# Other shapes for the paired tiles of a decoder trunk: halves and steps of 256, -64 and 64 bytes

## The chip, the cores and the metric

The kernel runs on one core of a Trainium2 chip. The metric is the device time of one execution in microseconds (us). Times are medians of several runs; the profile comes from one more execution, whose own time is given beside its span.

## What is computed

The reference is a decoder trunk of two layers over 256 tokens of width 2048. Each layer has a token mixer (a convolution module in the first, stick-breaking attention with 16 heads in the second) and a gated network with a causal depthwise convolution of width 3. Cut to what matters:

```python
def stick_breaking_mixer(h, qkv_w, o_w):
    ...
    o = stick_breaking_attention(qkv[0], qkv[1], qkv[2])
    o = o.transpose(0, 2, 1, 3).reshape(bsz, t_len, d)
    return o @ o_w

def conv_ffn(h, up_w, dw_w, dw_b, down_w):
    u = causal_depthwise_conv(h @ up_w, dw_w, dw_b)
    gt, val = jnp.split(u, 2, axis=-1)
    return (jax.nn.silu(gt) * val) @ down_w

def reference(x, c, ...):
    for i in range(DEPTH):
        ...
        x = x + gate * y
        ...
        x = x + gate * conv_ffn(h, ffn_up_w[i], ffn_dw_w[i], ffn_dw_b[i], ffn_down_w[i])
    return rms_norm(x, final_norm_g)
```

The inner width of the gated networks is 5632, that is 44 blocks of 128; the model width is 16 blocks of 128. All data are float32.

## The kernel before

Activations are kept transposed: a block is 128 channels (partitions) by 256 tokens. A product runs over a list of pairs (output block, inner block) in an order that `plan` writes out; weights come in pieces of 8 such blocks of 128 x 128 (`load_next`, a 512 KB DMA into `raw`), and `split_next` splits each piece into a rounded high part `wh` (ScalarE) and a remainder `wl` (VectorE), both in the type float32r that TensorE multiplies in one pass.

The activations are split in the same way into a high half and a low half. A product is then high x high + low x high + high x low. In `gemm` there are two forms. Without `both`, there are three matmuls of 256 columns for each weight block (L302 to L304). With `both`, the two halves of the activation tile are read as one moving operand of 2 x 256 columns against `wh` (L298), and the high half alone, 256 columns, against `wl` (L299): a pair. The weight block is loaded anew ahead of each matmul.

The halves lie in one tile. `h_tiles` and `halved` lay them out: `HP = T + 8 = 264` numbers from the start of one half to that of the next, 528 numbers (2112 bytes) for a tile. Four kinds of tiles come from `halved`: `z` (input of the second product of the convolution module, L943, read in triples), `g` of either network (input of the down products, L999), and `o` (one for each head, L1127). The `h` tiles come from `h_tiles`.

The g tiles of a network live in a pool of their own, opened in `ffn`, with 23 names (`NG = KF // 2 + 1`) for 44 inner blocks: block j takes the name `g{j % 23}`. Each network runs up product, down product over blocks 0 to 21, up product, down product over blocks 22 to 43. A down product runs over 16 output blocks; the plan begins with four output blocks in turn on each inner block (all but the last four inner blocks, which then come output block by output block), then takes the other twelve one at a time over all 22 inner blocks. The output projection `o` does the same over 16 inner blocks, one for each head. Tiles of one pool lie one behind the other in the order in which they are first taken.

The v product of the attention is written apart (`v_product`, L1164 to L1166): there the h tile is the stationary operand and 512 contiguous columns of `wh` or `wl` are the moving one.

While TensorE multiplies, VectorE splits weights (L247), closes each output block (L1010, L1012) and sums the conditioning matrices of the stages to come (L336), whose rows GpSimd's queue fetches (1 MB each).

Of the kernel before, what the change touches and what calls it, by code (L numbers as in the profile page):

```python
# [11 lines left out]
F32R = mybir.dt.float32r  # L12
# [4 lines left out]
P = 128  # L17
# [7 lines left out]
LATE_POOL, LATE_PE = 10, 8  # L25
PRODUCTS = 11

HEAD = 16
UBUFS = 9
M0 = 6  # L30
# [86 lines left out]
def hybrid_trunk(ctx: ExitStack, tc: tile.TileContext, cfg: Cfg, io: dict):  # L117
    nc = tc.nc
    D, T, H = cfg.D, cfg.T, cfg.H
# [253 lines left out]
    HP = T + 8  # L373
# [7 lines left out]
    def h_pairs():  # L381
        return [pairs[k] for k in range(KD)]

    def halved(pool, name):

        v = pool.tile([P, 2 * HP], F32R, name=name).rearrange("p (a t) -> p a t", a=2)[:, :, :T]
        return v[:, 0], v[:, 1], v

    def split_act(t, hh, hl, bias=None):
# [120 lines left out]
    with ExitStack() as cv:  # L510
# [422 lines left out]
        for j in range(KD + 1):  # L933
            if j < KD:
                zt.append(t256())
                if j > 1:
                    nc.vector.tensor_tensor(ys[j], ys[j], dm, op=ALU.subtract)
                nc.vector.tensor_tensor(zt[j], ys[j], rs, op=ALU.mult)
                nc.scalar.activation(zt[j], zt[j], AF.Silu, bias=pc("ln_b", j, 1), scale=pc("ln_g", j, 1))
            if j == 1:  # L940
                low()
            if j > 0:
                zs.append(halved(zpool, f"z{j - 1}"))  # L943
                split_act(zt[j - 1], *zs[j - 1][:2])
            if j in (1, 2, 4):
                split_next()
# [18 lines left out]
    def ffn(i, entry, out):  # L965
        m = f"ffn{i}"
        NG = KF // 2 + 1
        with ExitStack() as fs:
            gpool = fs.enter_context(tc.tile_pool(name=f"g{i}", bufs=1))
            if i == 0:  # L970
                more["pool"] = fs.enter_context(tc.tile_pool(name="mods", bufs=MORE_MODS))
            gh, gl, gb = [None] * KF, [None] * KF, [None] * KF
            pend = {}

            def conv3(ps, nb, both):
                y = t256()
                if both:
                    s = t256()
                    nc.scalar.copy(s, ps[:, T:2 * T])
                    nc.vector.tensor_tensor(s, ps[:, :T], s, op=ALU.add)  # L980
                    ps = s
                w = lambda k: pc(f"fdw{i}", nb * FW + k, 1)
                nc.scalar.activation(y, ps[:, :T], AF.Identity, bias=pc(f"fdb{i}", nb, 1), scale=w(FW - 1))  # L983
                for k in range(FW - 1):
                    s = FW - 1 - k
                    nc.vector.scalar_tensor_tensor(y[:, s:], ps[:, :T - s], w(k), y[:, s:],  # L986
                                                   op0=ALU.mult, op1=ALU.add)
                return y

            def up_done(nb, ps, both=False):  # L990
                pend[nb] = conv3(ps, nb, both)
                j = nb % KF
                if not (j in pend and j + KF in pend):
                    return
                yg, yv = pend.pop(j), pend.pop(j + KF)
                s = t256()
                nc.scalar.activation(s, yg, AF.Silu)
                nc.vector.tensor_tensor(s, s, yv, op=ALU.mult)
                gh[j], gl[j], gb[j] = halved(gpool, f"g{j % NG}")  # L999
                nc.scalar.copy(gh[j], s)  # L1000
                nc.vector.tensor_tensor(gl[j], s, gh[j].bitcast(F32), op=ALU.subtract)

            def down_done(h):
                def done(nb, ps):
                    if nb < KD - 2:
                        t = t256()
                        nc.scalar.activation(t, ps[:, T:2 * T], AF.Copy, scale=gate(m, nb))  # L1007
                        nc.gpsimd.tensor_tensor(xs[nb], xs[nb], t, op=ALU.add)  # L1008
                    else:
                        nc.vector.scalar_tensor_tensor(xs[nb], ps[:, T:2 * T], gate(m, nb), xs[nb],  # L1010
                                                       op0=ALU.mult, op1=ALU.add)
                    nc.vector.scalar_tensor_tensor(xs[nb], ps[:, :T], gate(m, nb), xs[nb],  # L1012
                                                   op0=ALU.mult, op1=ALU.add)
                    if h == 1 and i == 0:
                        out.add(nb)
                    elif h == 1:
                        out.add(xs[nb])
                        nc.scalar.activation(xs[nb], xs[nb], AF.Copy, scale=pc("fin_g", nb, 1))
                return done

            hh, hl = entry.product(f"up{i}0a", up_done, "silu_and_others")
            both = h_pairs() if i else None
            rest = (lambda nb, ps: up_done(nb, ps, True)) if i else up_done
            gemm(f"up{i}0b", hh, hl, rest, banks=[psum_b, psum_a], both=both)
            gemm(f"up{i}1a", hh, hl, rest, both=both)
            need(m, 2)
            gemm(f"down{i}0", gh, gl, down_done(0), both=gb)
            gemm(f"up{i}1b", hh, hl, rest, both=both)
            act_tables("sqrt_and_others")
            gemm(f"down{i}1", gh, gl, down_done(1), quiet=QUIET, both=gb)  # L1030
            drain(fill)
# [37 lines left out]
    with ExitStack() as at:  # L1069
# [12 lines left out]
        def attention(h):  # L1082
            q, k, v, vc = qk[h], qk[H + h], vs[h // GH], (h % GH) * P
            yield
            zp = (psum_acc if h == 1 else psum_a)()
            nc.tensor.matmul(zp[:, 0:T], k[:, 0:P], q, start=True, stop=True)
            nc.tensor.matmul(zp[:, T:CO], k[:, P:2 * P], q[:, P:2 * P], start=True, stop=True)
            z = zp[:, :CO]
            e = t2.tile([P, CO], F32, name="e", bufs=3)
            nc.scalar.activation(e, z, AF.Abs)  # L1090
            nc.scalar.activation(e, e, AF.Exp, scale=-1.0)
            lg = t2.tile([P, CO], F32, name="lg")
            nc.scalar.activation(lg, e, AF.Ln, bias=one_c)
            mk = t2.tile([P, CO], F32, name="e", bufs=3)
            nc.vector.scalar_tensor_tensor(mk, z, 0.0, lg, op0=ALU.max, op1=ALU.add)
            nc.vector.scalar_tensor_tensor(lg, z, 0.0, lg, op0=ALU.min, op1=ALU.subtract)
            for c0 in (0, T):
                nc.gpsimd.affine_select(out=mk[:, c0:c0 + P], in_=mk[:, c0:c0 + P], pattern=[[1, P]],
                                        compare_op=ALU.is_gt, fill=0.0, base=0, channel_multiplier=-1)
            if h < 2:  # L1100
                yield
            mh = t2.tile([P, CO], F32R, name="mh", bufs=1)
            ml = t2.tile([P, CO], F32R, name="ml", bufs=1)
            yield
            with tc.high_priority(offset=PRIORITY):
                nc.scalar.copy(mh, mk)
                nc.vector.tensor_tensor(ml, mk, mh.bitcast(F32), op=ALU.subtract)
            yield
            yield
            sp = psum_b()  # L1110
            nc.tensor.matmul(sp[:, :CO], tri_r, mh, start=True, stop=False)
            nc.tensor.matmul(sp[:, :CO], tri_r, ml, start=False, stop=False)
            nc.tensor.matmul(sp[:, P:T], ones_r, mh[:, T:CO], start=False, stop=False)
            nc.tensor.matmul(sp[:, P:T], ones_r, ml[:, T:CO], start=False, stop=True)
            nc.vector.tensor_tensor(lg, lg, sp[:, :CO], op=ALU.subtract)
            a = t2.tile([P, CO], F32, name="e", bufs=3)
            nc.scalar.activation(a, lg, AF.Exp)
            for c0 in (0, T):
                nc.gpsimd.affine_select(out=a[:, c0:c0 + P], in_=a[:, c0:c0 + P], pattern=[[1, P]],
                                        compare_op=ALU.is_gt, fill=0.0, base=0, channel_multiplier=-1)  # L1120
            yield
            yield
            op = psum_b()
            nc.tensor.matmul(op[:, 0:P], v[:, 0, vc:vc + P], a[:, 0:P], start=True, stop=True)
            nc.tensor.matmul(op[:, P:T], v[:, 0, vc:vc + P], a[:, P:T], start=True, stop=False)
            nc.tensor.matmul(op[:, P:T], v[:, 1, vc:vc + P], a[:, T:CO], start=False, stop=True)
            oh[h], ol[h], ob[h] = halved(apool, f"o{h}")  # L1127
            with tc.high_priority(offset=PRIORITY):
                nc.scalar.copy(oh[h], op[:, :T])
                nc.vector.tensor_tensor(ol[h], op[:, :T], oh[h].bitcast(F32), op=ALU.subtract)  # L1130
# [210 lines left out]
```

## Time and profile before

| | |
|---|---|
| time, median of 3 runs | 2302.11 us (2302.03 to 2304.25) |
| time of the profiled execution | 2302.23 us |
| its span, first to last instruction | 2300.5 us |
| matmuls in the trace | 14378 |
| L298 on h, g, o tiles | 1760, 1408, 256 |
| L299 on h, g, o tiles | 1760, 1408, 256 |
| DMA | 603.14 MB, mean 262 GB/s |

How to read it: PE is TensorE's matmuls, PEld its weight loads, DVE VectorE, ACT ScalarE, POOL GpSimd, SP the engine that issues the weight DMAs. Rows of groups and of windows give busy time and counts. The duration that the profile gives for one matmul covers more than the distance to the next one's start, as matmuls overlap in the array; the distance from start to start is what adds up to the time of a stage. A row such as "387/394/406" gives the shortest, the median and the longest duration in ns. A row of the windows view begins with the stretch in us from the start of the span and its length, then busy time and count for each engine asked for, the granted clock, the share of the DMA engines' time and GB/s.

### The profile page before, as it was taken

Reading aid. Unit: us, or ns where it says so; the run is one execution under the profiler, and the core shown is the slowest. Engines: PE = TensorE matmul, PEld = TensorE weight load, DVE = VectorE, ACT = ScalarE, POOL = GpSimd, SP = SyncE. Lnnn points to the kernel's source line nnn. Section 1 sums busy time; section 2 is a strip of 40 time slices with the busy share of each in tenths; the row PEclk is TensorE's granted clock in tenths of the full one; section 3 lists DMA queues with packets and bytes.
Section 4 is the critical chain, followed back from the end, with each engine's and each line's share of the span. In section 5 each row is a group of like instructions: output and inputs, shape, how many; then the busy total and the mean of one; then the engine's idle time right before and its main releaser. Section 6 shows DMA issues by size and latency. Waiting matters only on the chain.

```text
span 2300.5 us, 37664 instructions
## 1 busy us (share of the span) xinstructions
PE 2266.0 (98%) x14378; PEld 2012.9 (87%) x14378; DVE 1791.2 (78%) x2508; ACT 1219.9 (53%) x1930; POOL 406.2 (18%) x534
## 2 busy tenths in 40 slices
PE   7999999999999999999999999999999999999997
PEld 5888678999998999998888888888888888888886
DVE  7689968889998899999975555779899655777654
ACT  2056655755544455555465555657555544555553
POOL 4058713200003100003311100112000010000031
PEclk9999999999999999999999999999999999999999
DMA  9988799788899989898755555566777666666663
GB/s 396 416 327 311 268 368 361 267 301 336 332 339 347 332 329 343 334 332 320 265 184 160 165 173 171 168 188 234 240 281 275 194 191 186 190 184 191 189 188 110
DMA packets 139143, 603.14 MB, mean 262 GB/s; under 512 B 15441, under 2 KB 15569, under 8 KB 115153
## 3 DMA queue, kind: packets, MB, share of 16 engines
q1 hardware_dynamic: 120242, 464.42, 57.9%
q0 software_dynamic: 18720, 136.32, 16.0%
q8 instruction: 112, 1.84, 0.3%
q14 instruction: 69, 0.57, 0.1%
HBM read 598.58 MB, written 2.10 MB: 261 GB/s over the span
## 4 chain that ended last, share of the span: by engine, by line
PE 88%; DVE 5%; DMA 4%; ACT 1%; issue 1%; POOL 0%; DVEq 0%; SPq 0%; ACTq 0%; POOLq 0%
PE ps L298 33%; PE ps L299 17%; PE ps L302 9%; PE ps L303 8%; PE ps L304 8%; PE ps L678 5%; DMA mraw<-in_mt_mix 3%; DVE mraw L336 2%; DVE wl L247 1%; PE ps L1164 1%; PE ps L1165 1%; PE ps L1166 1%; PE ps L591 1%; PE auxa L591 1%; DMA mraw<-in_mt_ffn 1%
## 5 line engine op out<-in xcount | busy, mean ns | idle before, releaser
L247 DVE TENSOR_TENSOR wl<-raw,wh 128x1024 fp32r<-128x1024 f32 x688 | 849.0, 1241 | 297.7 <-ACT wh L243 295.9
L243 ACT CAST wh<-raw 128x1024 fp32r<-128x1024 f32 x688 | 719.3, 1047 | 661.7 <-PE ps L298 301.6
L298 PE MATMUL ps<-h,wh 128*128 128x512 f32 x1760 | 619.0, 394 | 0.0
L299 PE MATMUL ps<-h,wl 128*128 128x256 f32 x1760 | 493.7, 281 | 0.0
L298 PE MATMUL ps<-g,wh 128*128 128x512 f32 x1408 | 493.2, 394 | 0.0
L302 PE MATMUL ps<-h,wh 128*128 128x256 f32 (+1 forms) x1504 | 421.7, 280 | 0.0
L303 PE MATMUL ps<-h,wh 128*128 128x256 f32 (+1 forms) x1504 | 420.5, 280 | 0.0
L304 PE MATMUL ps<-h,wl 128*128 128x256 f32 (+1 forms) x1504 | 419.0, 279 | 0.1
L299 PE MATMUL ps<-g,wl 128*128 128x256 f32 x1408 | 395.3, 281 | 2.4 <-DVE wl L247 2.2
L298 PEld LDWEIGHTS ps<-h,wh 128*128 128x128 f32 x1760 | 330.5, 188 | 74.4
L336 DVE CUSTOM_DVE_ANT_0 mraw<-mraw,csr 128x2048 f32<-128x2048 f32 x152 | 348.7, 2294 | 42.4 <-DMA mraw<-in_mt_mix 31.0
L299 PEld LDWEIGHTS ps<-h,wl 128*128 128x128 f32 x1760 | 332.3, 189 | 0.2
L298 PEld LDWEIGHTS ps<-g,wh 128*128 128x128 f32 x1408 | 264.3, 188 | 60.4
L303 PEld LDWEIGHTS ps<-h,wh 128*128 128x128 f32 x1504 | 284.7, 189 | 0.1
L304 PEld LDWEIGHTS ps<-h,wl 128*128 128x128 f32 x1504 | 282.6, 188 | 0.7 <-DVE wl L247 0.7
L302 PEld LDWEIGHTS ps<-h,wh 128*128 128x128 f32 x1504 | 282.4, 188 | 0.2
L299 PEld LDWEIGHTS ps<-g,wl 128*128 128x128 f32 x1408 | 265.9, 189 | 4.0 <-DVE wl L247 4.0
L678 PE MATMUL ps<-h,raw 128*128 128x256 f32 x832 | 188.8, 382 | 0.0
L678 PEld LDWEIGHTS ps<-h,raw 128*128 128x128 f32 x832 | 157.8, 191 | 28.3 <-issue 6.7
L1008 POOL TENSOR_TENSOR x<-x,t 128x256 f32<-128x256 f32 x56 | 68.1, 1218 | 534.6 <-ACT t L1007 534.5
L986 DVE SCALAR_TENSOR_TENSOR t<-t,par 128x254 f32<-128x254 f32 (+1 forms) x184 | 88.8, 483 | 46.6 <-ACT t L983 43.7
L718 DVE SCALAR_TENSOR_TENSOR auxb<-u,cpar,auxb 128x256 f32<-128x256 f32 x297 | 121.6, 482 | 4.5 <-ACT auxb L702 3.8
(266 smaller groups left out, 2613.3 us busy)
## 6 DMA issues: line engine op xcount, KB each, us to landing
raw<-in_w_down SPq DMA_DIRECT2D x176, 512.0 KB, 4.4
mraw<-in_mt_ffn POOLq DMA_DIRECT2D x64, 1024.0 KB, 6.1
raw<-in_w_pw SPq DMA_DIRECT2D x96, 512.0 KB, 8.1
mraw<-in_mt_mix POOLq DMA_DIRECT2D x48, 1024.0 KB, 7.9
raw<-in_w_up01b SPq DMA_DIRECT2D x84, 512.0 KB, 6.2
raw<-in_w_up11b SPq DMA_DIRECT2D x84, 512.0 KB, 3.8
raw<-in_w_up00b SPq DMA_DIRECT2D x80, 512.0 KB, 6.2
raw<-in_w_up10b SPq DMA_DIRECT2D x80, 512.0 KB, 4.7
```

What stands on the lines that cost most here:

```text
L243: nc.scalar.copy(wh[:, :n], v[:, :n])
L247: nc.vector.tensor_tensor(wl[:, :n], v[:, :n], wh[:, :n].bitcast(F32), op=ALU.subtract)
L298: nc.tensor.matmul(o, wh[:, c], both[kt], start=first, stop=False, skip_group_check=True)
L299: nc.tensor.matmul(o[:, :T], wl[:, c], xh[kt], start=False, stop=left[nb] == 0, skip_group_check=True)
L302: nc.tensor.matmul(o, wh[:, c], xh[kt], start=first, stop=False, skip_group_check=halves > 0)
L303: nc.tensor.matmul(o, wh[:, c], xl[kt], start=False, stop=False, skip_group_check=halves > 0)
L304: nc.tensor.matmul(o, wl[:, c], xh[kt], start=False, stop=left[nb] == 0, skip_group_check=halves > 0)
L336: nc.vector.tensor_tensor_reduce(out=v, in0=v, in1=csr, scale=1.0, scalar=0.0, op0=ALU.mult, op1=ALU.add, accum_out=macc[:, nb:nb + 1])
L678: nc.tensor.matmul(banks[j][:, nb // KD * T:(nb // KD + 1) * T], w[:, b * P:(b + 1) * P], hf[kt], start=first, stop=left[j] == 0, skip_gro ...
L718: nc.vector.scalar_tensor_tensor(conv_ps[j], us[j % UBUFS][:, k:k + T], tap(j, k), conv_ps[j], op0=ALU.mult, op1=ALU.add)
L986: nc.vector.scalar_tensor_tensor(y[:, s:], ps[:, :T - s], w(k), y[:, s:], op0=ALU.mult, op1=ALU.add)
L1008: nc.gpsimd.tensor_tensor(xs[nb], xs[nb], t, op=ALU.add)
```

## The change

`halved` takes its shape from a table by kind: the distance between the halves, the size of the tile, both in numbers of 4 bytes, and how many numbers are left free ahead of the first tile of that kind. `z` keeps its numbers. `g0` (first network) has halves 256 apart in tiles of 512, with 24 left free ahead of the first; `g1` (second network) halves 264 apart in tiles of 560; `o` (heads) halves 272 apart in tiles of 544. What is written into the tiles, and what reads them, is the same.

```diff
+PAIRS = {"z": (264, 528, 0), "g0": (256, 512, 24), "g1": (264, 560, 0), "o": (272, 544, 0)}
...
-    def halved(pool, name):
-
-        v = pool.tile([P, 2 * HP], F32R, name=name).rearrange("p (a t) -> p a t", a=2)[:, :, :T]
+    ahead_of = {kind: v[2] for kind, v in PAIRS.items()}
+
+    def halved(pool, kind, name):
+
+        low, size, _ = PAIRS[kind]
+        at = ahead_of.pop(kind, 0)
+        v = pool.tile([P, at + size], F32R, name=name)[:, at:at + 2 * low].rearrange("p (a t) -> p a t", a=2)[:, :, :T]
         return v[:, 0], v[:, 1], v
...
-                zs.append(halved(zpool, f"z{j - 1}"))
+                zs.append(halved(zpool, "z", f"z{j - 1}"))
...
-                gh[j], gl[j], gb[j] = halved(gpool, f"g{j % NG}")
+                gh[j], gl[j], gb[j] = halved(gpool, f"g{i}", f"g{j % NG}")
...
-            oh[h], ol[h], ob[h] = halved(apool, f"o{h}")
+            oh[h], ol[h], ob[h] = halved(apool, "o", f"o{h}")
```

## The prediction, made before the changed kernel was built or run

> **What bounds the kernel now.** I read the page first (span, busy shares, chain), then busy time by stage, and then single matmul starts, since only those are finer than the change.
>
> ```profile
> span 2300.5 us, 37664 instructions
> PE 2266.0 (98%) x14378; PEld 2012.9 (87%) x14378; DVE 1791.2 (78%) x2508; ACT 1219.9 (53%) x1930; POOL 406.2 (18%) x534
> PEclk9999999999999999999999999999999999999999
> PE 88%; DVE 5%; DMA 4%; ACT 1%; issue 1%; POOL 0%; DVEq 0%; SPq 0%; ACTq 0%; POOLq 0%
> ```
>
> TensorE works for 98% of the span, at full granted clock in every slice, and holds 88% of the chain that ended last. Time can only fall if its matmuls start closer together. The profiled execution took 2302.23 us around its 2300.5 us span, 0.12 us over the median of the runs shown, so I sum against 2302.23 and subtract 0.12 at the end.
>
> The stages that the change touches are the two down products of the first network (rows 1 and 3 below), the output projection o of the heads (row 4) and the two down products of the second network (rows 5 and 7). Rows 2 and 6 are up products, whose h tiles stay as they are.
>
> ```profile
> core 0: us, PE busy (x) PEld busy (x) DVE busy (x) ACT busy (x) POOL busy (x), PEclk, DMA share, GB/s
> 668.14:791.33 123.19, 123.19 (x706) 107.97 (x705) 104.72 (x105) 53.51 (x61) 28.10 (x33) 1.00 0.94 348
> 791.33:1026.57 235.24, 235.24 (x2018) 235.24 (x2017) 216.91 (x276) 123.20 (x180) 16.40 (x31) 1.00 0.89 332
> 1026.57:1153.46 126.89, 124.50 (x706) 107.99 (x705) 118.47 (x131) 64.11 (x94) 43.88 (x41) 1.00 0.80 292
> 1452.90:1545.30 92.40, 92.40 (x534) 81.16 (x533) 68.93 (x86) 55.32 (x77) 19.26 (x20) 1.00 0.60 183
> 1805.48:1928.70 123.22, 123.22 (x707) 108.00 (x706) 64.03 (x67) 53.66 (x62) 14.18 (x14) 1.00 0.64 192
> 1928.70:2163.90 235.20, 235.20 (x1347) 206.35 (x1346) 169.34 (x249) 133.73 (x206) 0.00 (x0) 1.00 0.62 188
> 2163.90:2287.11 123.21, 123.21 (x706) 108.06 (x705) 59.52 (x62) 63.51 (x90) 28.41 (x28) 1.00 0.50 154
> ```
>
> A down product is 16 output blocks by 22 inner blocks, so 352 pairs of one 512-column matmul (L298, joined halves against wh) and one 256-column matmul (L299, first half against wl): 704 matmuls. 123.2 us over 352 pairs is **350.0 ns a pair**. The up product of row 6 has 42 blocks by 16, so 672 pairs in 235.20 us: 350.0 again. That of row 2 has three 256-column matmuls in place of a pair, 672 triples in 235.24 us: 350.1. So 768 columns cost 350 ns whether they come as two matmuls or three, from h or from g. The first reading is discouraging for this change: on average the time goes by columns.
>
> **Addresses do matter locally.** A joined tile is 2 x 264 numbers, 2112 bytes, which is 64 modulo 256: each next inner block starts 64 bytes further round a circle of 256. From the program's memory plan the first g tile starts at 160 modulo 256, then 224, 32, 96, 160.
>
> ```profile
> L298 PE MATMUL ps<-g,wh x1408: 387/394/406, 668.1 to 2286.8; 128*128 128x512 f32 x176
> 1808.30:1809.73 1.43, 1.43 (x11) 1.00 0.87 301
> 1809.73:1811.13 1.40, 1.40 (x11) 1.00 0.86 319
> 1811.13:1812.52 1.39, 1.39 (x11) 1.00 0.13 53
> 1812.52:1813.93 1.41, 1.41 (x11) 1.00 0.76 186
> ```
>
> The first row: the same matmul takes 387 to 406 ns. The other four are stretches of four pairs each on one tile, at 32, 96, 160 and 224 (a down product begins with four output blocks in turn on each inner block): 357.5, 350, 347.5 and 352.5 ns a pair. So a fixed address repeated has its own price, a few ns either side of 350. The DMA share runs from 0.13 to 0.87 across them without order, so transfers are not what differs.
>
> **The change part by part.** No instruction, wait or DMA is added, removed or moved; z keeps its numbers. What changes is where the g and o tiles lie, hence the price of 704 pairs with g of the first network, 704 of the second and 256 of o (16 blocks by 16). 1 ns on all 1664 pairs is 1.66 us.
>
> First network: joined halves are contiguous, tiles 2048 bytes, start 0 modulo 256 (24 numbers are put ahead of the first tile; when that name is used again in the second product it is not, a 22nd of that stage, counted like the rest). Every step from block to block is then 0 modulo 256. Nearest rows: the v product, whose moving operand is a contiguous 512 columns of wh or wl, always the same modulo 256.
>
> ```profile
> 1231.36 0.39 PE L1166 MATMUL ps<-wh,h 128*128 128x512 f32 x1
> 1231.59 0.39 PE L1164 MATMUL ps<-wh,h 128*128 128x512 f32 x1
> 1231.82 0.40 PE L1165 MATMUL ps<-wl,h 128*128 128x512 f32 x1
> 1232.05 0.39 PE L1166 MATMUL ps<-wh,h 128*128 128x512 f32 x1
> 1232.29 0.59 PE L1086 MATMUL auxa<-q,k 128*128 128x256 f32 x2
> ```
>
> Four starts in 0.93 us: 232.5 ns for 512 columns, 348.8 for 768, 1.2 under 350. Over 704 pairs **-0.8 us**. Bounds from the fixed-address rows: 347.5 (-1.8 us) to 357.5 (+5.3 us). I take the v rows because they alone are contiguous.
>
> Second network: tiles of 560 numbers, 2240 bytes, -64 modulo 256; halves as before. The trace has that step once per output block, at the return from the last inner block (224) to the first (160):
>
> ```profile
> 1805.48:1830.78 25.30, 25.30 (x145) 1.00 0.67 207
> 1836.38:1921.00 84.62, 84.62 (x486) 1.00 0.64 188
> 2194.79:2279.42 84.63, 84.63 (x487) 1.00 0.51 156
> 1851.41 0.39 PE L298 MATMUL ps<-g,wh 128*128 128x512 f32 x1
> ...
> 1851.76 0.40 PE L298 MATMUL ps<-g,wh 128*128 128x512 f32 x1
> ...
> 1852.12 0.39 PE L298 MATMUL ps<-g,wh 128*128 128x512 f32 x1
> ...
> 1852.46 0.39 PE L298 MATMUL ps<-g,wh 128*128 128x512 f32 x1
> ```
>
> The second row holds 11 whole output blocks, 242 pairs; at 350.0 it would be 84.70. It is 0.08 us short, so each of 11 steps of -64 is worth some **-6 to -7 ns** over what follows it (in the head, first row, 72 pairs with steps of 0 in 25.30 us, 351.4, the price is over 350 instead). In single starts the gain is not at the step: the pair right after it takes 0.36, the next 0.34. I carry it over as if each step were worth it: some 273 more such steps in the first down product and 268 in the second (every inner step of the twelve single output blocks, one in four in the head), 541 x 6.3 ns = **-3.4 us**. Bounds: nothing recurring (0), or the 0.36 pair at every step (read to 0.01, so between 0.35 and 0.36: +5 ns each, +2.7 us).
>
> Heads: tiles of 2176 bytes, step 128, halves 1088 bytes apart in place of 1056. The second down product of the second network goes 160, then 32, then 160 on its return (two steps of 128): 84.63 against 84.70 over 11 returns, 22 steps, -3.2 ns each; o takes some 219 such steps: **-0.7 us**. That halves 64 apart cost otherwise than halves 32 apart no row shows; ends 347.5 and 357.5 a pair give -0.6 to +1.9 us, and I take 0, because the contiguous v rows (0 apart) and the h rows (32 apart) differ by only 1.2.
>
> Whether the rest keeps up: the fullest of these stages is the second of the first network, where VectorE works 118.47 of 126.89 us and TensorE already stood still.
>
> ```profile
> PE ps L299 <- DVE wl L247: 2.2, 3, 1.1
> 1084.18 10.04 DMA mraw<-in_mt_ffn
> L1000 ACT CAST g<-t x88: 390/407/413, 440.6 to 2169.3; 128x256 fp32r<-128x256 f32 x88
> L1001 DVE TENSOR_TENSOR g<-t,g x88: 416/420/427, 441.3 to 2170.3; 128x256 fp32r<-128x256 f32 x88
> ```
>
> A 10 us transfer on the chain holds VectorE, and wl comes late three times; a faster TensorE arriving there earlier would wait longer by what it gained, at most half of the 0.8 us. In the other four stages VectorE is busy for 85% or less. The writers of the moved tiles (L1000, L1001, 0.4 us each, and the like for o) I cost at nothing: they finish well ahead of the down product that reads them, beside matmuls; if each were a tenth slower, 88 x 0.08 = 7 us on two engines with room, not on the chain.
>
> Sum: -0.8 - 3.4 - 0.7 = -4.9; 2302.23 - 4.9 - 0.12 = **2297.2 us**, 0.2% down, at the very edge of what a measurement of this kernel can tell from no change (about 0.2%, 4.6 us).
>
> [...]
>
> [...]
>
> **The rivals.**
> *Fixed by columns.* The local differences are only displaced starts that even out, as 350.0 in three kinds of stage suggests. For it: the stage rows. Against: 357.5 beside 347.5 at fixed addresses, and 242 pairs 0.08 us short twice. **2302.1 us**, band 2 us. [...]
>
> *Pieces of 64 bytes.* If the moving operand is fetched in 64-byte pieces at a fixed price, a pair before touches 17 + 16 + 17 = 50 (halves start at 32 and 0 modulo 64), so 7.0 ns each. The new first network touches 32 + 16 = 48: 336 ns, -14 x 704 = -9.9 us; o touches 51: +7 x 256 = +1.8; the second network 50. With the steps' -3.4: **2290.6 us**. For it: v touches 33 pieces, 231 against 232.5 seen. Against: nothing decisive; the aligned half of h (L303) shows no shorter stage.
>
> *A bad address.* The new address 0 lies between 224 (352.5) and 32 (357.5) in the fixed-address rows, and after the change every one of the 704 pairs repeats it. If it locks in as 32 does, +7.5 x 704 = +5.3 us, and if the -64 step keeps its 0.36 pairs, +2.7: 2302.1 + 8.0 = **2310.1 us**. It makes the kernel slower by over 0.2% once the mean pair exceeds 350 + 4.6/1.664 = 352.8. For it: 1.43. Against: the v rows, fixed at one address and contiguous, at 348.8.
>
> **How the numbers follow.** Forecast 0.42, band 2294.5 to 2300, of which 0.24 lies under 2297.5; fixed by columns 0.22; 64-byte pieces 0.22; bad address 0.14. Faster 0.24 + 0.22 = 0.46, same 0.18 + 0.22 = 0.40, slower 0.14. The range 2288 to 2306.5 leaves out most of the bad address (0.12) and the low end of the pieces (0.05).
>
> **What would show it.** Forecast: first network's down products near 348.8 ns a pair (122.8 us and, with its waits, about 126.5), second network's near 121.5 us each, o near 91.7, up products unchanged at 235.2. Columns: all at 350.0. Pieces: first network 118.3 us a product. Bad address: 125.8 us there. It would be wrong altogether if an up product changed, if the number of matmuls changed, or if VectorE's wait in the second down product grew by more than the stage gained.

## The result, and the profile after

The changed kernel takes 2305.97 us (median of 18 runs, lowest 2304.56) against 2302.70 us for the kernel before (18 runs): ratio 1.0015, 95% interval 1.0009 to 1.0021. One of the 18 runs of either kernel took 3200 us (its granted clock in the changed kernel's was 0.66); without it the medians are 2305.93 and 2302.66. The changed kernel is slower by 0.15%, inside what I had called no change (0.2%), and on the other side of the forecast of 2297.2 us.

First the page of the changed kernel: its span, the busy shares and the granted clock.

```profile
span 2304.9 us, 37664 instructions
PE 2270.7 (99%) x14378; PEld 2015.0 (87%) x14378; DVE 1791.1 (78%) x2508; ACT 1222.4 (53%) x1930; POOL 406.0 (18%) x534
PEclk9999999999999999999999999999999999999999
```

Instructions and matmuls are what they were; the granted clock was 0.997 over the span, 0.998 before; TensorE is busy for 4.7 us more (2270.7 against 2266.0). The profiled execution took 2306.58 us, the one of before 2302.23 us. Next the windows view of the changed kernel, the same seven stages as before in the same order (the columns: stretch, length, TensorE's busy time and matmuls, granted clock, DMA share, GB/s; all windows rows below have them).

```profile
core 0: us, PE busy (x), PEclk, DMA share, GB/s
669.50:793.90 124.40, 124.40 (x707) 1.00 0.93 346
793.90:1029.10 235.20, 235.20 (x2019) 1.00 0.89 331
1029.10:1156.40 127.30, 125.47 (x707) 1.00 0.80 291
1455.70:1548.10 92.40, 92.40 (x536) 1.00 0.60 183
1808.30:1932.30 124.00, 124.00 (x706) 1.00 0.63 191
1932.30:2167.50 235.20, 235.20 (x1346) 1.00 0.62 188
2167.50:2291.50 124.00, 124.00 (x706) 1.00 0.51 153
```

The up products (rows 2 and 6) have not moved. All four down products have become longer. With the stage bounds taken from the start times of single matmuls, to the nanosecond:

| stage | before, us | after, us | after, ns a pair |
|---|---|---|---|
| first network, first down product | 123.19 | 124.38 | 353.35 |
| first network, second | 126.89 | 127.28 | 352.6 without its waits |
| o | 92.43 | 92.35 | 350 |
| second network, first | 123.22 | 123.97 | 352.2 |
| second network, second | 123.22 | 124.03 | 352.4 |

Together +1.19 + 0.39 - 0.08 + 0.75 + 0.81 = +3.06 us, which is the difference of the medians (3.3 us) within its interval. The two profiled spans differ by 4.4; the other 1.4 us lie before the first down product (669.5 against 668.1), where nothing was changed. There the granted clock of the changed kernel's execution fell for a moment; of the kernel before it was 1.00 in both stretches:

```profile
352.00:356.00 4.00, 2.98 (x18) 0.76 1.01 416
356.00:360.00 4.00, 4.00 (x23) 0.82 0.85 305
```

That is 4 x 0.24 + 4 x 0.18 = 1.7 us of clock, an estimate from these two rows, and in a run below with the same first network the product starts at 668.0.

In the first down product all operands now stand at one address modulo 256, and yet the pairs are not alike. These are the starts of the matmul with the joined halves in the timeline of the changed kernel:

```profile
729.93 0.40 PE L299 MATMUL ps<-g,wh 128*128 128x512 f32 x1
...
730.29 0.39 PE L299 MATMUL ps<-g,wh 128*128 128x512 f32 x1
...
730.64 0.40 PE L299 MATMUL ps<-g,wh 128*128 128x512 f32 x1
...
731.00 0.39 PE L299 MATMUL ps<-g,wh 128*128 128x512 f32 x1
...
731.34 0.40 PE L299 MATMUL ps<-g,wh 128*128 128x512 f32 x1
...
731.70 0.39 PE L299 MATMUL ps<-g,wh 128*128 128x512 f32 x1
```

0.36, 0.35, 0.36, 0.34, 0.36: to the nanosecond one pair takes 240 + 121 = 361 and the next 229 + 117 = 346, through the whole stage. Equal work at an equal address settled into a rhythm of two pairs. That is the first sign that the time of a pair is not a property of its own address alone.

### The profile page after: what moved, and what is told of

Its sections match the earlier page's. It is cut to its first block, busy times and chain, and to the rows that moved or that the text cites. A ratio compares the mean times of both kernels' runs of the same rounds, so it can differ in the third digit from the quotient of the medians.

```text
span 2304.9 us, 37664 instructions
## 1 busy us (share of the span) xinstructions
PE 2270.7 (99%) x14378; PEld 2015.0 (87%) x14378; DVE 1791.1 (78%) x2508; ACT 1222.4 (53%) x1930; POOL 406.0 (18%) x534
## 4 chain that ended last, share of the span: by engine, by line
PE 88%; DVE 5%; DMA 4%; ACT 1%; issue 1%; POOL 0%; DVEq 0%; SPq 0%; POOLq 0%; ACTq 0%
PE ps L299 33%; PE ps L300 17%; PE ps L303 9%; PE ps L304 8%; PE ps L305 8%; PE ps L683 5%; DMA mraw<-in_mt_mix 3%; DVE mraw L337 2%; DVE wl L248 1%; PE ps L1170 1%; PE ps L1171 1%; PE ps L1169 1%; PE ps L596 1%; PE auxa L596 1%; DMA mraw<-in_mt_ffn 0%
## 5 line engine op out<-in xcount | busy, mean ns | idle before, releaser
L299 PE MATMUL ps<-h,wh 128*128 128x512 f32 x1760 | 619.0, 394 | 0.0
L299 PE MATMUL ps<-g,wh 128*128 128x512 f32 x1408 | 496.9, 396 | 0.0
L299 PEld LDWEIGHTS ps<-h,wh 128*128 128x128 f32 x1760 | 330.4, 188 | 74.4
L299 PEld LDWEIGHTS ps<-g,wh 128*128 128x128 f32 x1408 | 264.4, 188 | 63.6
```

The source lines that it names most:

```text
L299: nc.tensor.matmul(o, wh[:, c], both[kt], start=first, stop=False, skip_group_check=True)
```

## The experiments

My theory after the result, R: a pair's price is set by where the moving operand (g, o, h) stands to the weight block loaded beside it, modulo 256 bytes, and repeats in a short cycle. The rivals: A, the operand's own address sets it; J, joining the halves, at any address, costs 3.35 ns a pair; C, the columns alone set it. Open besides: how much of the joined matmul's time goes with reading the operand's columns, and how much with reading those of the weights. In the tables of shapes below the three numbers are the distance of the halves, the size of the tile and what is left free ahead; an edit that begins with such a table is one of the changed kernel. Stage times and prices of a pair come from the one profiled execution of each run. The weight blocks stand at 32 modulo 256 unless they are moved; "stand" means operand minus weights. The steady cycle is what repeats in the twelve single output blocks, where each tile is followed by the next.

**Weights moved, operands left** (one run). The kernel before, with two pools opened in the other order, so that wh and wl stand at 160 and no operand moves.

```diff
-    w_pool = ctx.enter_context(tc.tile_pool(name="wsplit", bufs=4))
     tmp = ctx.enter_context(tc.tile_pool(name="tmp", bufs=2))
+    w_pool = ctx.enter_context(tc.tile_pool(name="wsplit", bufs=4))
```

> The kernel before, with the split weights (wh, wl) 128 bytes further on modulo 256 and every activation tile where it was. Theory R (relation): a pair's price is set by where its moving operand stands to the weights modulo 256. Then the prices of the four fixed-address stretches at the head of the second network's first down product change places: 1.39 us at address 32 (it was 1.43), 1.41 at 96 (1.40), 1.43 at 160 (1.39), 1.40 at 224 (1.41). Theory A (own address): the moving operand's own address and step set the price: 1.43, 1.40, 1.39, 1.41 at 32, 96, 160, 224 as before. Theory C (columns): the local prices even out whatever lies where: stages at 350.0 ns a pair. All three: total within 0.1% of before.

2303.47 us, against 2302.39 for the kernel before. The windows view of this run, for the four stretches of four pairs that the prediction quoted, on tiles at 32, 96, 160 and 224:

```profile
1809.23:1810.62 1.39, 1.39 (x11) 1.00 0.64 253
1810.62:1812.02 1.40, 1.40 (x10) 1.00 0.94 275
1812.02:1813.45 1.43, 1.43 (x11) 1.00 0.38 155
1813.45:1814.85 1.40, 1.40 (x10) 1.00 0.78 199
```

Before, the tile at 32 was the dear one (1.43) and that at 160 the cheap one (1.39). Now it is the other way round, with the operands where they were. In the steady cycle every address shows what the address 128 further showed before (32: 225 + 119, was 234 + 119; 160: 234 + 119, was 225 + 119). A is refuted, R holds for the prices at each address. It does not give the sum: two of the four down products took 123.54 and 123.55 us (before 123.19 and 123.22). An output block there takes 7720 ns, before 7693; the part on why the prediction was wrong comes back to it.

**The change, moved as a whole** (one run). Weights and the g and o tiles of the changed kernel all 128 bytes further; the weights by the order of the two pools, as above.

```diff
-PAIRS = {"z": (264, 528, 0), "g0": (256, 512, 24), "g1": (264, 560, 0), "o": (272, 544, 0)}
+PAIRS = {"z": (264, 528, 0), "g0": (256, 512, 56), "g1": (264, 560, 32), "o": (272, 544, 32)}
```

> The changed kernel with weights and all its g and o tiles moved on together by 128 bytes modulo 256 (h and z stay). Relation theory: stage times of the changed kernel to 0.1 us: 124.4 and about 127.3 us in the first network, 124.0 twice in the second, o 92.35. Own address: the prices change with the addresses (128 in place of 0 for the first network).

2304.82 us against 2302.35. The first down product:

```profile
668.00:792.36 124.36, 124.36 (x707) 1.00 0.94 346
```

The same 361 and 346 in turn. o took 92.36 us, the second network 123.98 us and then 123.62, where the change itself has 124.03. The first network's second product took 127.59 us, the change's 127.28. Stands alone give the price to 0.1 us in three of the five; the second network's second product ran in another rhythm.

**The first network's shape alone** (five rounds).

```diff
+PAIRS = {"z": (264, 528, 0), "g0": (256, 512, 24), "g1": (264, 528, 0), "o": (264, 528, 0)}
```

> Only the first network's shape of the change (joined halves, multiples of 256), the second network and the heads as before. From the stages of the changed kernel: its two down products cost 1.2 and 0.4 us more, second network and o 0: in all +1.6 us, ratio 1.0007 to 1.001. The prediction's own term for this part: -0.8 us, ratio 0.9996.

2304.14 against 2302.47 us, ratio 1.0007, interval 0.9998 to 1.0016: by itself not told from no change. Its stages tell: 124.38 and 127.26 us in the first network (together +1.56), 123.22 twice in the second, o 92.44. This shape acts in its own stages and nowhere else.

**One stand for every block** (one run). Tiles of 576 numbers, 2304 bytes, so that every step is 0 modulo 256, halves 32 apart as before: first network at 160 (128 from the weights), second at 32 (0), o at 96 (64).

```diff
+PAIRS = {"z": (264, 528, 0), "g0": (264, 576, 0), "g1": (264, 576, 32), "o": (264, 576, 48)}
```

> Halves 264 numbers apart as before, but every tile of a kind at one address modulo 256 (tiles of 2304 bytes, steps of 0): first network's g at 160, second network's g at 32, o at 96. R and A: the prices of the fixed-address stretches of before hold for whole stages: first network 347.5 ns a pair (122.3 us a product), second network 357.5 (125.8 us a product), o 350 (92.4 us). In total 3 to 4 us over before. C: 350.0 ns in all of them and the time of before.

2304.16 against 2302.39 us. The first down products of the two networks and the second of the second:

```profile
668.10:790.13 122.03, 122.03 (x706) 1.00 0.94 351
1803.00:1928.55 125.55, 125.55 (x707) 1.00 0.61 189
2163.70:2289.10 125.40, 125.40 (x707) 1.00 0.50 152
```

346.7 ns a pair at a stand of 128, 356.7 and 356.1 at 0, and o 350.0 at 64. One shape, three prices, by the stand. These are the fixed-address prices of before made permanent.

**Joined halves** (one run). The change's first shape (halves 256 apart, tiles of 512) in all three places, at the stands of the run above.

```diff
+PAIRS = {"z": (264, 528, 0), "g0": (256, 512, 0), "g1": (256, 512, 32), "o": (256, 512, 48)}
```

> Halves joined without a gap (256 numbers apart, tiles of 2048 bytes, steps of 0) as in the first network of the changed kernel, but at other addresses modulo 256: first network's g at 160, second network's at 32, o at 96. If joining the halves is what costs (theory J): pairs alternate near 346 and 361 ns at every address, 353.3 on average, 124.4 us a down product, o near 93.2 us. If the address decides (R, A): 347.5 at 160, 357.5 at 32, 350 at 96, that is 122.3 and 125.8 us a product, o 92.4. C: 350.0 throughout.

2301.88 against 2302.39 us. The two down products of the second network, one layout, one set of instructions:

```profile
1805.40:1927.44 122.04, 122.04 (x707) 1.00 0.63 194
2162.60:2286.76 124.16, 124.16 (x706) 1.00 0.50 154
```

The first runs at 230 + 117 = 346.7 ns for every pair, the second in a cycle of three (232 + 118, 241 + 120, 236 + 113; 352.7 over the product). In the first network (stand 128) it is 351.1, in o (stand 64) 353.1. J, one price for joining, is refuted. Something else appears: one layout stayed for a whole product in one rhythm (346.7) and for the next in another (352.7).

**Steps and halves apart from each other** (one run). First network in steps of 128 with halves 32 apart; second in steps of 64 with halves 64 apart; o in steps of -64.

```diff
+PAIRS = {"z": (264, 528, 0), "g0": (264, 544, 0), "g1": (272, 592, 0), "o": (264, 560, 0)}
```

> One property moved in each kind: first network's g with steps of 128 and halves 264 apart as before; second network's g with halves 272 apart (64 bytes in place of 32 modulo 256) and steps of 64 as before; o with steps of -64 and halves as before. The step theory of the prediction (-3.2 ns for each step of 128): first network 346.8 ns, 122.1 us a product. If a step of -64 costs what the second network of the changed kernel shows: o at 351.8 ns, 92.8 us. If the distance of the halves alone matters: second network off 350.0; if not, 123.2 us a product. C: 350.0 throughout.

2302.60 against 2302.39 us. The first down product of each network:

```profile
668.10:790.57 122.47, 122.47 (x707) 1.00 0.93 348
1804.40:1928.40 124.00, 124.00 (x707) 1.00 0.62 191
```

Where steps of 128 rule (the single output blocks of the first product), a pair takes 346.7: -3.3 for each step. Halves 64 apart in steps of 64: 352.2 and 352.0, so +2. Steps of -64 in o: 351.8, close to the changed kernel's second network (352.2).

**The low weights apart from the high ones** (one run). wl 128 bytes from wh, in a pool of its own.

```diff
+    wl_pool = ctx.enter_context(tc.tile_pool(name="wlow", bufs=4))
...
-        wl = w_pool.tile([P, PW], F32R, name="wl")
+        wl = wl_pool.tile([P, PW], F32R, name="wl")
```

> The kernel before with the low weights wl 128 bytes further on modulo 256 than the high weights wh. If the weight load that runs beside a matmul is what its operand collides with, then the joined matmul (beside it, wl is loaded) and the 256-column one (beside it, the next wh) no longer see the same relation, and the local prices change to values that were not seen before, with the stage averages off 350.0 by up to 3.5 ns either way (1.2 us a down product, 2.3 us an up product). If only the moving operand's own address counts: nothing changes.

2309.23 against 2302.35 us, the slowest of all. But the pairs hardly moved: 123.43 us for the first down product (350.65 a pair), 123.46 and 123.45 in the second network; only the pattern did (at 160, 230 + 115 in place of 225 + 119). The 7 us lie before the first down product (it starts at 671.7) and in the first network's second up product, 238.50 us in place of 235.24, the stretches in which h is read in triples. From the middle of that up product, in this run:

```profile
860.00:940.00 80.00, 80.00 (x679) 1.00 0.89 330
```

and in the kernel before:

```profile
860.00:940.00 80.00, 80.00 (x688) 1.00 0.92 341
```

TensorE waits for nothing there in either; it starts 679 matmuls in 80 us where it started 688. So the price of triples too changed with the place of the weights, and theirs was the better of the two before.

**One column for the operand** (one run). In the second network's down products the joined matmul reads one column of each half 256 times (the high weights' part of these two products is then not computed).

```diff
+            flat = lambda v: v[:, :, 0:1].to_broadcast([P, 2, T])
...
-both=gb
+both=[flat(v) if i and v is not None else v for v in gb]
```

> The kernel before, but in the second network's down products the joined matmul reads the first column of each half 256 times over in place of the 256 columns (so the high weights' part of these two products is not computed). [...]

2290.13 against 2302.35 us, down products of 117.48 and 117.53 us. Its timeline:

```profile
1860.16 0.38 PE L298 MATMUL ps<-g,wh 128*128 128x512 f32 x1
1860.38 0.28 PE L299 MATMUL ps<-g,wl 128*128 128x256 f32 x1
1860.50 0.38 PE L298 MATMUL ps<-g,wh 128*128 128x512 f32 x1
1860.72 0.28 PE L299 MATMUL ps<-g,wl 128*128 128x256 f32 x1
```

0.22 us from L298's start to L299's, to the nanosecond 215 at every address alike (mean 215.3). The 256-column matmul beside it, which still reads its whole operand, stays at 118. With as many columns multiplied, the joined matmul is some 16 ns shorter (before: 225 to 234 in the steady cycle, mean 231), so that much of it goes with reading the operand's columns.

**One column for the weights** (one run). In the same products every weight load reads one column 128 times (these two products are then not computed); the operands are read in full.

```diff
+                    cut = (lambda w: w[:, b * P:b * P + 1].to_broadcast([P, P])) if name[:5] == "down1" else (lambda w: w[:, c])
-                    nc.tensor.matmul(o, wh[:, c], both[kt], ...
+                    nc.tensor.matmul(o, cut(wh), both[kt], ...
-                    nc.tensor.matmul(o[:, :T], wl[:, c], xh[kt], ...
+                    nc.tensor.matmul(o[:, :T], cut(wl), xh[kt], ...
```

> The kernel before, but in the second network's down products every weight load reads one column 128 times over in place of 128 columns (so these two products are not computed). [...] If the operand's own reads are slow by themselves and the weights only shift them: no address pattern, but still near 233 and 117 ns, 123 us.

2300.94 against 2302.47 us; down products of 122.48 and 122.36 us. The four stretches on tiles at 32, 96, 160 and 224 again, in this run:

```profile
1808.58:1809.97 1.39, 1.39 (x11) 1.00 0.85 292
1809.97:1811.36 1.39, 1.39 (x11) 1.00 0.76 262
1811.36:1812.74 1.38, 1.38 (x10) 1.00 0.34 137
1812.74:1814.13 1.39, 1.39 (x10) 1.00 0.66 186
```

At fixed addresses the pattern is gone: 347.0 to 347.2 ns a pair at all four, where it was 346.0 to 357.0. In the single output blocks some of it stays. The first product has 347 to 349 there, by address (mean 348.2); the second still repeats 349, 348, 350 and 344 at 160, 224, 32 and 96, where it was 344, 350, 353 and 353. So most of the dependence on the stand goes with the reads of the weights' columns, not all of it: the spread between addresses fell from 11.0 to 0.2 ns at fixed ones, from 9 to 2 and 6 in the single output blocks. And with these reads reduced a pair still takes 348, against 333.8 in the run above: some 14 ns of it go with the operand's columns, and the reads of the weights shift the time by -1 to +10 ns at fixed stands.

**A stand of 128 for all three** (five rounds). Both networks and o with tiles of 576 numbers from 160.

```diff
+PAIRS = {"z": (264, 528, 0), "g0": (264, 576, 0), "g1": (264, 576, 0), "o": (264, 576, 0)}
```

> Every g and o tile at 160 modulo 256, which is 128 from the weights: halves 264 numbers apart, tiles of 2304 bytes, z and h as before. By the relation theory the 346.7 ns of the first network in the second experiment hold for both networks and the heads: 122.0 us a down product in place of 123.2 (the second of the first network 125.9 with its waits), o 91.5. Total 4.5 to 5.5 us under the kernel before, ratio 0.9977 to 0.998. Theory C (columns): no difference.

2299.64 against 2302.35 us, ratio 0.9989, interval 0.9980 to 0.9998: faster than both kernels, by a tenth of a per cent. The first down product of each network, and o:

```profile
668.10:790.13 122.03, 122.03 (x706) 1.00 0.93 350
1804.00:1926.06 122.06, 122.06 (x706) 1.00 0.63 194
1450.80:1543.77 92.97, 92.97 (x535) 1.00 0.59 181
```

The networks give their 346.7. o, in the same layout, got 349 in its first four output blocks and then locked into the slow rhythm, 232.5 + 121 = 353.3. The profiled execution, 2298.43 us, was 1.2 us faster than the median; what the others did stage by stage no trace shows.

**The best price for every paired tile** (five rounds). Networks as above, o and h in steps of 128; for its memory, the convolution module keeps eight tiles of its ring in place of nine.

```diff
+PAIRS = {"z": (264, 528, 0), "g0": (264, 576, 0), "g1": (264, 576, 0), "o": (264, 544, 0)}
-UBUFS = 9
+UBUFS = 8
-        v = hpool.tile([P, 2 * HP], F32R, name=f"h{i}")
+        v = hpool.tile([P, 2 * HP + 16], F32R, name=f"h{i}")
```

> The shapes that were cheapest so far, h included: g of both networks at 160 modulo 256 throughout (346.7 ns a pair seen), o and the 16 h tiles in steps of 128 with halves 264 numbers apart (347.0 ns seen once a product runs one output block at a time). To make room the convolution's ring of inputs has 8 tiles in place of 9. Relation theory: up products from 235.2 to about 233.3 us each (three kinds: triples and pairs alike, as both walk the same halves), down products 122.0, o near 91.8; in all 3300 pairs and triples of h at -3 ns, 10 us, plus 5 us of g and o: 2287 to 2291 us, ratio 0.994 to 0.995. Column theory: 2302.

2300.54 against 2302.47 us, ratio 0.9994, interval 0.9986 to 1.0003. Every pair did as hoped: 122.03 us a down product, o 91.87, the second network's up products 233.81 and 232.99 (before 235.94 and 235.20). But the first down product starts at 672.6 in place of 668.1, and the windows view of this run shows of the triples:

```profile
794.60:1034.30 239.70, 239.70 (x2019) 1.00 0.88 327
860.00:940.00 80.00, 80.00 (x676) 1.00 0.89 329
```

239.70 us in place of 235.24, with no wait of TensorE in it: the triples on h pay 4.5 us in the layout that suits the pairs, 356.7 ns each at both stands. The other 4.5, ahead of the first down product, stand beside the same waits of TensorE as before (1.6 us for t then, 2.0 now) and are dearer triples too: the 736 on h there take 264.5 us, before 260.2. Together that is nearly all of the 10 us that the pairs had gained.

**h by layer** (five rounds). As above, but in the first layer, where h is read in triples, the tiles meet the stands 0, 128, 64 and 192 in turn.

```diff
+    def h_tiles(i, m="0"):
+        v = hpool.tile([P, 2 * HP + 16], F32R, name=f"h{i}")
+        at = 16 * (i // 2 % 2) if m[-1] == "0" else 0
+        v = v[:, at:at + 2 * HP]
```

> Paired tiles as in e9_all_chosen (both networks always at 160, heads and h in tiles of 544 numbers), but in the first layer, where h is read in triples of 256 columns, every third and fourth h tile begins 64 bytes later, so that the triples meet the four stands 0, 128, 64, 192 in turn instead of 0 and 128 alone; in the second layer h stays in steps of 128. The pairs should be those of e9_all_chosen under every theory: 122.0 us a down product, 91.9 for o, 233.8 and 233.0 for the paired up products. What is open is why the gain of e9_all_chosen (some 9 us in its pairs) was given back before the first down product (+4.5 us) and in the triples of the first up product (239.7 against 235.2 us). If a triple's price is that of the stands that it meets, averaged, the triples go back to 235.2 us, the first down product begins near 668, and the whole takes about 2293 us, the fastest of all. If steps of 128 between neighbouring tiles cost the triples as such, nothing comes back: about 2300.5 us. If it was the ring of eight tiles in place of nine in the convolution module, the triples of the first up product go back to 235.2 or stay at 239.7 as above, but the 4.5 us ahead of the first down product stay: about 2297.

2303.47 against 2302.23 us, ratio 1.0005, interval 0.9996 to 1.0014. The first down product of each network and the triples between the first network's two:

```profile
672.00:796.38 124.38, 124.38 (x706) 1.00 0.92 345
1811.50:1933.53 122.03, 122.03 (x707) 1.00 0.63 194
796.40:1035.50 239.10, 239.10 (x2018) 1.00 0.88 326
```

Two misses. The triples stay at 239.1, though they meet the same four stands as in the kernel before, in another order (there 0, 64, 128, 192). So their price is not the mean of the stands that they meet. Whether it is the order, the tiles' new size or the ring of eight, which this run kept, was not isolated. And the first network, at the same stand and shape as in the last two runs, spent both its products in the slow rhythm (233 + 121, then twice 232 + 121, mean 353.3) in which o was caught before. Its two products are 2.35 and 1.77 us longer than in the run above (124.38 and 127.77 against 122.03 and 126.00); with 1.1 us less in and before the triples that makes 3.0 of the 3.1 us between the two profiled executions. This run was on another chip than the one above; the second network's products and o took there what they took in the run above, to 0.01 us.

## Why the prediction was wrong

What the runs show of a pair, in ns:

| stand of the operand to the weights | halves 32 bytes apart | joined |
|---|---|---|
| 128, always | 346.7, or 353.3 | 351.1 |
| 64, always | 350.0 | 353.1 |
| 0, always | 356.1 to 356.7 | 346.7, or 352.7 |
| 224, always (the change's first down product) | not run | 353.35 |
| steps of 64 (before; weights moved) | 350.0; 350.1 to 351.0 | not run |
| steps of -64 (the change's second network) | 351.8 to 352.4 | not run |
| steps of 128 | 346.7 | not run |

- **TensorE is the bound, and only starts of matmuls count: right.** The up products did not move, and the measured difference is that of the stages.
- **First network, -0.8 us: wrong, +1.6.** The step that failed is "I take the v rows because they alone are contiguous". That product is no fixed layout: its stationary operand is h, whose blocks go round the circle in steps of 64, so its 348.8 is a mean over stands: with the moving operand at one address, single ones of its matmuls take 224 to 241 ns from start to start as the h block changes. Contiguous halves have no price of their own (346.7 to 353.35 by stand and rhythm). My bounds, 347.5 to 357.5, did hold the 353.35.
- **Second network, -3.4 us: wrong, +1.6.** The step that failed is "I carry it over as if each step were worth it", and so did the reading under it, that the 0.08 us were the returns'. An output block has 22 inner blocks, five turns of the circle and two blocks over. The steady cycle (344, 350, 353 and 353 ns at 160, 224, 32 and 96) gives 5 x 1400 + 694 = 7694 ns, as the two over are the cheap ones; 7693.3 is measured. So the 0.08 us come from the count of blocks, and the return by -64 is worth under 1 ns. With the weights moved the two over are the dear ones (5 x 1400 + 706), and the return costs 14 ns besides: the 7720 above. Where each step is -64, another cycle settled (356, 345, 355 and 351 ns at stands 128, 64, 0 and 192, in the order of the blocks), 351.75 on average: +1.75 a step in place of -6.3. The upper end that I gave, +5 a step, contained it.
- **Heads, -0.7 us: -0.1.** The term of the steps came out: -3.3 each where only the step was changed, and 91.87 us for o with halves 32 apart in steps of 128 (-0.56). Failed is "I take 0" for halves 64 apart: by themselves they cost some +2, and the two together measured 349.9. That the term came out is in part luck: of the 6.7 ns an output block that I shared between two steps of 128, the count of blocks explains 3 (7697 by the cycle, 7693.3 measured, 7700 at 350.0 a pair).
- **Fixed by columns: refuted.** 350.0 in three kinds of stage was no law of columns. All of them had steps of 64 past weights at one address, and so the pairs on g, o and h the same four prices to 1 ns, 353 + 353 + 344 + 350: I read one layout's mean several times as so many witnesses. The triples had four others (352, 348, 351 and 349); that they too averaged 350.1 was chance, and 355 to 357 in three other layouts.
- **Pieces of 64 bytes: refuted** by 353.35 where it wanted 336.
- **A bad address: right in place, too large.** The pairs of the first down product do repeat one cycle, but 3.35 ns over, where I had put 7.5; and the address by itself does not make the price.
- **VectorE's wait** (the time of the first network's second product over its pairs' price) went from 3.73 to 3.18 us, and to 4.00 where that product became faster (the run with all at a stand of 128). A slower TensorE that comes later to it would do that; it is not shown, as single executions spread as far (the product took 126.89 us before and 126.13 in the one-column run, which left it as it was).

Three runs bear on the reads. The joined matmul takes 225 to 244 ns in the kernel before (99% of them), and 215.3 where it read one column of each half. With the weights moved by 128 bytes the dear address moved by 128, and with one column read for them the prices at the four fixed addresses became one (347.0 to 347.2).

What stays open: how the reads of the operand and those of the weights bear on each other, what chooses between two rhythms of one layout, and what the triples want. The last two decide whether a better layout than that of 0.9989 can be had.

## What to carry to other kernels

Where TensorE starts back to back and equal matmuls differ from start to start (here 225 to 244 ns for 512 columns), the addresses of the moving and the stationary operand against each other are worth a look, in a run in which only the weights move. A price read at one step or one address is not to be multiplied into a stage whose whole train (the row of operands one after another) has that step: test the train. Before a few ns are put down to a step, count whether the stretch holds whole cycles of the prices that are known. And a layout is to be timed in every form in which the tile is read, since the layout that made pairs 1% faster (350.0 to 346.7 ns) made triples 2% slower (350.1 to 356.7).

## What the hardware showed

- The time of a pair went with where the moving operand stands to the weights modulo 256 bytes: 346.7 ns at a stand of 128, 350.0 at 64 and 356.1 to 356.7 at 0, halves 32 apart. With the weights' reads reduced to one column it was 347 at each of four fixed addresses, but still 344 to 350 in one train of steps of 64.
- The joined matmul took 215.3 ns where it read one column of each half, and about 231 where it read all 512, also when the weight loads read one column.
- Equal instructions on equal addresses held one of at least two rhythms through a product of 352 pairs: 346.7 or 353.3 ns (halves 32 apart, stand 128), 346.7 or 352.7 (joined, stand 0). This alone moved one product by 2.1 to 2.35 us.
